# A decoder layer on one core: the input projection by seven half-size products, in a phase of its own

## The chip, the core and the metric

The kernel runs on one core of a Trainium2 chip. A core has five engines, each with its own instruction queue: TensorE (PE) for matmuls, with its weight loads as PEld; VectorE (DVE), ScalarE (ACT) and GpSimd (POOL) for work on 128 partitions; SyncE (SP), which here issues nearly all transfers between DRAM and the on-chip memory (SBUF), in order. An instruction waits on semaphores at the head of its engine's queue, and all that is queued behind it on that engine waits too. Matmuls write into banks of PSUM. The metric is the time of one execution on the device, in microseconds; lower is better.

## The reference

One layer for 1024 tokens of width 1024, all in fp32. `c` gives shifts, scales and gates; the mixer's input projection makes 62 chunks of 128 columns; two kinds of attention follow, gated branches, an output projection, layer norm, and a feed-forward part.

```python
u = x * (1.0 + scale_m) + shift_m
proj = einsum('btd,de->bte', u, w_in)              # 1024 x 1024 by 1024 x 7936
qa, ka, va, qb, kb, vb, ga, gb = split(proj)       # A: 16 query, 2 key/value heads; B: 3 groups of 8 heads
qa, ka, qb, kb = rope(...)                         # rotary embedding
oa = banded_window_attention(qa, ka, va, 127, sinks)
for g, (window, dil) in enumerate(((128, 1), (512, 4), (2048, 16))):
    o_g, lse_g = dilated_attention(q_g, k_g, v_g, window, dil)
ob = sum over g of softmax(lse)[g] * o_g
y  = (sigmoid(ga) * (oa @ w_branch_a) + sigmoid(gb) * (ob @ w_branch_b)) @ w_o
x  = layer_norm(alpha * x + (1 + gate_m) * y)
h  = (x * (1 + scale_f) + shift_f) @ w_gate_up     # then silu(hg) * hu, @ w_down
x  = layer_norm(alpha * x + (1 + gate_f) * ...)
```

## The kernel before

**Products.** TensorE takes fp32 numbers as a rounded part and a remainder ("hi" and "lo"). A product of two such numbers is three matmuls, hi·hi, hi·lo and lo·hi (`mac`, L136 to L139). A weight piece of 128x512 is loaded (`w_raw`, L55), copied to `w_hi` by ACT (L78) and its remainder `w_lo` made by DVE (L79). A chunk of the input projection is 8 slices of the inner dimension by two halves of the tokens by three: 48 matmuls with 512 columns.

**Prologue** (to about 72 us). It makes `u` from x as eight pairs of tiles, and the first three chunks (`EARLY`) beside it.

**Phase 1** (72 to about 834 us). Twenty units of attention, 12 of kind B (pair of heads p, group g with strides 1, 4, 16) and 8 of kind A, each in four sub-steps. `stream` yields the projection of the keys, values and queries of each unit in small pieces, and `pump` and `at` place these between the attention's instructions on PE so that a unit's projection runs while the unit before it attends. Rope is in `rotary`: a product with the cosines (DVE, L422), a shuffle (DVE, L423), a product with the sines and an addition that also reorders the columns by residue (POOL, L425, L426). `q_stacks` and `k_stacks` then write the hi and lo parts to partitions 0 to 63 and 64 to 127. Scores are L501 and L507, exponentials L528, transposes of the probabilities L550 with their copies L552, weighing of values L573. Results go to DRAM; group weights and row sums come back as broadcasts into `wb` by loads over 64 partitions each (`fetch_bcast`, L615).

**Phase 2** (to about 1117 us). Twenty-four branch steps (three blocks of eight columns chunks), between them 14 of 16 gates made by projection (`make_gate`, in a list `order`); two gates were made at the end of phase 1 and kept in DRAM (`ga_d`). One step of `ada` a branch step or gate forms later shifts and gates on DVE (`acc`, L826). Then the merged result `m` is split, in three blocks.

**The rest.** A pass over w_o, layer norm, and the feed-forward part. Its first projection already runs as seven products of half-size matrices per pair of chunks: `g_sums` forms sums of weight halves on POOL (L1080 to L1086), `g_split` makes their hi and lo parts, `product` (L1106) issues 12 matmuls, and the results are added.

The lines that the change rests on in PE's and SP's order:

```python
ends = np.cumsum(lengths)
at = lambda x: pump(min(int(start + (stop - start) * (i + x) / 4), total - 1))
scores(un, qr); at(0.4); turn_probs(*subs[s - 1]); exponentials(*subs[s]); at(0.8); weigh(...)
```

## Time and profile before

| what | value |
|---|---|
| times of two runs | 1898.89 and 1903.19 us, median 1901.04 |
| profiled execution: its own time | 1908.77 us |
| its span, first to last instruction | 1907.0 us |
| mean granted TensorE clock | 0.987 |
| PE busy | 1841.1 us (97%) |
| DVE busy | 1160.4 us (61%) |
| ACT busy | 782.0 us (41%) |
| POOL busy | 596.5 us (31%) |
| DMA | 170.83 MB, mean 90 GB/s |

"Busy" is the time in which an engine has an instruction of its own under way; what a busy PE does is not told by it. An idle stretch of PE is put down to what released the waiting instruction. A row of groups reads: line, engine, operation, tiles written <- read, shapes, count, then busy time in all, mean nanoseconds of one, idle time of the engine just before them with the releaser. In a table of windows each row gives start and end in microseconds, the length, each engine's busy time with its number of instructions, the granted clock (PEclk, 1.00 is full), the busy share of the 16 DMA engines and the rate. In a timeline the figures are start and duration, both in microseconds. Matmuls overlap, so their pitch is shorter than the duration of one.

### The profile page before, as it was taken

To read this page: it belongs to the slowest core of one execution; us is meant where nothing else is said; L and a number is where in the kernel's file an instruction comes from. 1 tells how busy PE (TensorE), PEld (TensorE's weight loads), DVE (VectorE), ACT (ScalarE), POOL (GpSimd) and SP (SyncE) were. 2 spreads that over 40 slices of the span, in tenths; PEclk is the share of its full clock that TensorE was granted. 3 is DMA by queue.
4 is the path that set the end of the run, shared out by engine and by line. 5 is a ranking of instruction groups with operands and counts; after the bars stand their busy time and mean duration, and the time that the engine had idled before them with its cause. 6 is when DMAs were issued, how large, how long until landed. Compare 5 with 4: busy or idle time off the path is not lost.

```text
span 1907.0 us, 24471 instructions
## 1 busy us (share of the span) xinstructions
PE 1841.1 (97%) x8988; PEld 1489.6 (78%) x8988; DVE 1160.4 (61%) x2161; ACT 782.0 (41%) x1661; POOL 596.5 (31%) x389
## 2 busy tenths in 40 slices
PE   6899999999999999989999999999999999899998
PEld 5688877878878777768888878778888888788886
DVE  7855667667677887534555364575565444565557
ACT  3455545445444767633122132653333333412122
POOL 2432223223323222100311142455664333431213
PEclk9899999999999999989999999999999999999999
DMA  8011112111121122254534123123222222432222
GB/s 316 28 34 34 40 41 74 45 57 56 41 63 50 53 89 68 79 178 164 175 118 161 56 75 124 56 89 100 89 78 89 78 89 95 135 125 90 93 71 89
DMA packets 72266, 170.83 MB, mean 90 GB/s; under 512 B 13073, under 2 KB 14161, under 8 KB 72146
## 3 DMA queue, kind: packets, MB, share of 16 engines
q1 hardware_dynamic: 71810, 168.21, 26.7%
q8 instruction: 71, 1.16, 0.3%
q0 software_dynamic: 336, 1.06, 0.2%
q14 instruction: 49, 0.40, 0.1%
HBM read 145.80 MB, written 23.43 MB: 89 GB/s over the span
## 4 chain that ended last, share of the span: by engine, by line
PE 51%; DVE 3%; ACT 1%; issue 1%; DMA 1%; SPq 0%; POOL 0%; DVEq 0%; ACTq 0%; POOLq 0%
PE pf L1106 21%; PE p L138 5%; PE p L139 5%; PE p L137 5%; PE pf L137 5%; PE pf L139 5%; PE pf L138 5%; DVE m L118 1%; DMA h_raw<-h_d 0%; DVE wd L79 0%; DVE h L118 0%; DMA oa_d<-o 0%; PE px L1034 0%; PE p L835 0%; PE p L842 0%
## 5 line engine op out<-in xcount | busy, mean ns | idle before, releaser
L137 PE MATMUL pj<-u,w_hi 128*128 128x512 f32 x720 | 301.5, 419 | 0.0
L139 PE MATMUL pj<-u,w_lo 128*128 128x512 f32 x720 | 283.9, 394 | 0.0
L138 PE MATMUL pj<-u,w_hi 128*128 128x512 f32 x720 | 282.6, 392 | 0.0
L425 POOL TENSOR_TENSOR rb<-rb,sin_t 128x512 f32<-128x512 f32 x64 | 86.8, 1356 | 502.0 <-DVE rb L423 431.5
L118 DVE TENSOR_TENSOR w_lo<-r,w_hi 128x512 fp32r<-128x512 f32 x110 | 117.7, 1072 | 138.7 <-ACT w_hi L117 137.9
L79 DVE TENSOR_TENSOR w_lo<-w_raw,w_hi 128x512 fp32r<-128x512 f32 x150 | 133.4, 893 | 85.3 <-ACT w_hi L78 83.0
L528 ACT ACTIVATE probs<-probs,st 128x128 f32<-128x128 f32 (+1 forms) x320 | 146.0, 461 | 60.5 <-DVE st L518 30.8
L137 PEld LDWEIGHTS pj<-u,w_hi 128*128 128x128 f32 x720 | 136.4, 189 | 33.6 <-issue 4.7
L139 PEld LDWEIGHTS pj<-u,w_lo 128*128 128x128 f32 x720 | 135.8, 189 | 30.7
L138 PEld LDWEIGHTS pj<-u,w_hi 128*128 128x128 f32 x720 | 136.7, 190 | 22.6
L137 PE MATMUL pf<-wd,h 128*128 128x512 f32 x352 | 139.2, 395 | 3.4 <-DVE zt L1326 2.9
L138 PE MATMUL pf<-wd,h 128*128 128x512 f32 x352 | 138.7, 394 | 1.9 <-DVE wd L79 1.9
L139 PE MATMUL pf<-wd,h 128*128 128x512 f32 x352 | 138.6, 394 | 0.0
L62 POOL TENSOR_TENSOR w_raw<-w_raw,gate 128x512 f32<-128x512 f32 x60 | 83.1, 1404 | 157.0 <-DMA w_raw<-in_w_down 134.4
L1326 DVE SCALAR_TENSOR_TENSOR zt<-zt,pf 128x512 f32<-128x512 f32 x112 | 76.2, 685 | 85.1 <-PE pf L139 85.0
L426 POOL TENSOR_TENSOR r<-ra,rb 128x512 f32<-128x512 f32 x63 | 114.5, 1817 | 6.1 <-DVE kl L460 1.3
L78 ACT ACTIVATE w_hi<-w_raw 128x512 fp32r<-128x512 f32 x150 | 92.0, 624 | 29.0 <-PE p L138 12.0
L552 ACT ACTIVATE ptsb<-pt 128x512 f32<-128x512 f32 (+1 forms) x128 | 63.6, 548 | 93.6 <-PE pt L550 93.2
L137 PE MATMUL p<-u,w_hi 128*128 128x512 f32 x224 | 88.3, 394 | 0.0
L139 PE MATMUL p<-u,w_lo 128*128 128x512 f32 x224 | 87.2, 389 | 0.0
L138 PE MATMUL p<-u,w_hi 128*128 128x512 f32 x224 | 87.2, 389 | 0.0
L137 PE MATMUL p<-o_hl,w_hi 128*128 128x512 f32 x192 | 75.9, 395 | 8.0 <-ACT o_hl L117 8.0
(297 smaller groups left out, 4267.2 us busy)
## 6 DMA issues: line engine op xcount, KB each, us to landing
w_raw<-in_w_in SPq DMA_DIRECT2D x118, 256.0 KB
r<-in_w_gate_up SPq DMA_DIRECT2D x47, 512.0 KB
a_raw<-in_w_ada SPq DMA_DIRECT2D x32, 512.0 KB
w_raw<-in_w_down SPq DMA_DIRECT2D x44, 256.0 KB
h_raw<-h_d SPq DMA_DIRECT2D x22, 512.0 KB
h_d<-g SPq DMA_DIRECT2D x40, 256.0 KB
wa<-in_w_ada_m SPq DMA_DIRECT2D x16, 512.0 KB
wb<-wt_d SPq DMA_DIRECT2D x24, 256.0 KB
```

Source lines behind the costliest of these rows:

```text
L62: self.nc.gpsimd.tensor_tensor(self.raws[i], self.raws[i], scale(), op=OP.mult)
L78: self.nc.scalar.activation(hi, raw, AF.Copy)
L79: self.nc.vector.tensor_tensor(lo, raw, hi, op=OP.subtract)
L118: nc.vector.tensor_tensor(lo, src, hi, op=OP.subtract)
L137: nc.tensor.matmul(ps, w[0], m[0], start=first, stop=False)
L138: nc.tensor.matmul(ps, w[0], m[1], start=False, stop=False)
L139: nc.tensor.matmul(ps, w[1], m[0], start=False, stop=last)
L425: eng.tensor_tensor(b, b, sin_t[:, s], op=OP.mult)
L426: eng.tensor_tensor(residue_half(res, r, t), by_residue(a, r), by_residue(b, r), op=OP.add)
L528: nc.scalar.activation(pr, pr, AF.Exp, bias=st[:, 0, h, b:b + 1], accum_out=st[:, 1, h, b:b + 1])
L1106: nc.tensor.matmul(ps, w[:, c], m[:, k], start=first and k == 0 and n == 0, stop=k == 3 and n == 2, skip_group_check=True)
L1326: nc.vector.scalar_tensor_tensor(z, z, ALPHA if gi == 0 else 1.0, pd, op0=OP.mult, op1=OP.add)
```

## The change

The 59 chunks of the input projection that follow the three early ones are taken apart from attention. Of them 52 are made in pairs by the seven products (a class `SevenProducts`, which the feed-forward part now shares): with the inner dimension and the tokens halved, seven products of 12 matmuls replace 96 matmuls by 84 for each pair of chunks. The operands made from `u` (sums and differences of its quarters: t1 to t4) are formed from x, which is loaded once more after the prologue, and split into hi and lo (`split_to`). One chunk of a pair (`ea`) is always a query or key chunk; the other a value or a gate chunk, or in five pairs another query or key chunk. Hi and lo parts of queries and keys (`hl_d`), the values (`v_d`) and nine gates (`ga_d`) are written to DRAM.

Then the attention phase begins. For each unit the query stacks (four loads of 64x1024), key stacks (four of 64x1024), the keys' remainders and the values are loaded, one unit ahead. Six gates are still made in full, woven between its sub-steps (48 pieces over 80 sub-steps), for which a quarter of `u` is formed once more. Probabilities are turned two sub-steps later instead of one, values weighed three later instead of two, and the PSUM banks are shared out anew. The last gate is made at the start of the branch phase, which otherwise has only the 24 branch steps, each with two steps of `ada`; gates are loaded, and `m` is split column chunk by column chunk in the last steps.

What moves in POOL's queue, in the kernel before, in the middle of phase 1 (`rb` and `ra` are the parts of rope, `r` its result):

```order
L426 TENSOR_TENSOR r<-ra,rb 128x16x32
L425 TENSOR_TENSOR rb<-rb,sin_t 128x512
L426 TENSOR_TENSOR r<-ra,rb 128x512
L425 TENSOR_TENSOR rb<-rb,sin_t 128x512
L426 TENSOR_TENSOR r<-ra,rb 128x512
```

And in the changed kernel, in one pair of the input phase; `half` and `row` are parts and results of rope, the tiles named r_ are raw weights and s_ their sums (957 and 959 of one pair, 1128 and 1130 of the next):

```order
L125 TENSOR_TENSOR s_1089<-s_1088,r_957 128x512
L591 TENSOR_TENSOR row<-half 128x512
L127 TENSOR_TENSOR r_959<-r_957,r_959 128x512
L531 TENSOR_TENSOR half<-half,sin_t 128x512
L534 TENSOR_TENSOR row<-half 128x16x32
L531 TENSOR_TENSOR half<-half,sin_t 128x512
L534 TENSOR_TENSOR row<-half 128x16x32
L123 TENSOR_TENSOR s_1259<-r_1130 128x512
L129 TENSOR_TENSOR r_957<-r_957,s_1089 128x512
L125 TENSOR_TENSOR s_1260<-s_1259,r_1128 128x512
```

POOL had only rope there; now the weight sums of the next pair and the fourth sum of the present one (L129) stand behind two halves of rope.

SP's queue in phase 1 of the kernel before, between two units (`st_d`, `cst` and `wb` carry group weights):

```order
L615 DMA wb<-wt_d 64x1024 x2
L55 DMA w_raw<-in_w_in 128x512
L664 DMA ob_d<-o 128x1024
L55 DMA w_raw<-in_w_in 128x512 x3
L590 DMA st_d<-sr 32x128
L55 DMA w_raw<-in_w_in 128x512 x6
```

And in the changed kernel where the input phase ends and attention begins (`qs`, `kh`, `kl`, `v` are the loads of the first unit, `ut` the quarter of x, `w_raw` the weights of the first woven gate):

```order
L503 DMA hl_d<-row 128x1024
L504 DMA hl_d<-row 128x1024
L627 DMA qs<-hl_d 64x1024
L628 DMA qs<-hl_d 64x1024
L627 DMA qs<-hl_d 64x1024
L628 DMA qs<-hl_d 64x1024
L615 DMA kh<-hl_d 64x1024 x4
L620 DMA kl<-hl_d 128x1024
L632 DMA v<-v_d 128x1024
L915 DMA ut<-in_xT 128x512 x4
L55 DMA w_raw<-in_w_in 128x512 x6
```

SP carried only weights there; now the first unit's ten loads stand behind the last stores, and the weights of the gate, with which PE's instructions of the new phase begin, behind those.

The diff, cut to its core:

```diff
+PRODUCTS = ("b11", "b21", "t2", "t1", "t3", "b22", "t4")
...
+class SevenProducts:
...
+    def load(self, p, both=True):
+        got = []
+        for i, src in enumerate(self.sources[p][:1 + both]):
+            got.append(self.pool.tile([P, T], F32, name=f"r{i + 1}", bufs=2))
+            self.nc.sync.dma_start(got[i], src)
+        self.raws[p] = got
+    def sums(self, p, step):
+        r1, r2 = self.raws[p]
+        tt = self.nc.gpsimd.tensor_tensor
+        if step == 0:
+            self.s[p] = [self.pool.tile([P, 512], F32, name=n, bufs=1) for n in ("s1", "s2")]
+            tt(self.s[p][0], r2[:, H0], r2[:, H1], op=OP.add)
+        elif step == 1:
+            tt(self.s[p][1], self.s[p][0], r1[:, H0], op=OP.subtract)
+        elif step == 2:
+            tt(r2[:, H0], r1[:, H0], r2[:, H0], op=OP.subtract)
+        else:
+            tt(r1[:, H1], r1[:, H1], self.s[p][1], op=OP.subtract)
+    def split(self, p, i):
+        raw = self.raws[p]
+        src = (raw[0][:, H1] if i in (1, 5) else raw[0][:, H0] if i == 0 else self.s[p][3 - i] if i in (2, 3) else
+               raw[1][:, H0 if i == 4 else H1])
+        hi, lo = [self.wpool.tile([P, 512], F32R, name=n, tag=n, bufs=4) for n in ("w_hi", "w_lo")]
+        self.split_(hi, lo, src)
+        self.ready.append((hi, lo))
+    def prepare(self, upto):
+        while self.prepared < min(upto, len(self.jobs)):
+            p, i = self.jobs[self.prepared]
+            if i == 5:
+                self.sums(p, 3)
+            self.split(p, i)
+            self.prepared += 1
+    def product(self, ps, i, first):
+        hi, lo = self.ready.pop(0)
+        b = self.B[PRODUCTS[i]]
+        for k in range(4):
+            c = slice(k * P, (k + 1) * P)
+            for n, (w, m) in enumerate(((hi, b[0]), (hi, b[1]), (lo, b[0]))):
+                self.nc.tensor.matmul(ps, w[:, c], m[:, k], start=first and k == 0 and n == 0,
+                                      stop=k == 3 and n == 2, skip_group_check=True)
...
-    tail_gates = (4, 5)
-    for e in range(EARLY, 46):
+    rope_chunks = [e for e in range(EARLY, 36) if e % 3 != 1] + [36] + list(range(38, 46))
+    other_chunks = [e for e in range(EARLY, 36) if e % 3 == 1] + [37] + list(range(46, 55))
+    pairs = []
+    while rope_chunks:
+        pairs.append((rope_chunks.pop(0), other_chunks.pop(0) if other_chunks and len(pairs) % 5 != 4
+                      else rope_chunks.pop(0)))
+    assert not other_chunks
+    woven_gates, last_gate = list(range(55, 61)), 61
+    for e in woven_gates + [last_gate]:
...
+    hl_d = dram.tile([46, 2, P, T], F32, name="hl_d")
+    v_d = dram.tile([13, P, NB, P], F32, name="v_d")
...
+    t_half = slice(TH, T)
+    for name in ("t2", "t1", "t4"):
+        operand(name, low1)
+    raw_t3 = [row() for _ in range(2)]
+    for k in range(4):
+        uab = []
+        for j in (k, k + 4):
+            x_t = row()
+            nc.sync.dma_start(x_t, I["xT"][j])
+            u_again(x_t, x_t, j, 0)
+            uab.append(x_t)
+        if k == 1:
+            inp.load(0)
+        ua, ub = uab
+        t3 = raw_t3[k // 2][:, (k % 2) * TH:(k % 2 + 1) * TH]
+        nc.gpsimd.tensor_tensor(t3, ub[:, t_half], ua[:, t_half], op=OP.subtract)
+        nc.vector.tensor_tensor(ua[:, t_half], ua[:, t_half], ua[:, :TH], op=OP.subtract)
+        nc.vector.tensor_tensor(ua[:, :TH], ub[:, t_half], ua[:, t_half], op=OP.subtract)
+        nc.vector.tensor_tensor(ub[:, :TH], ub[:, :TH], ua[:, :TH], op=OP.subtract)
+        for name, src in (("t2", ua[:, :TH]), ("t1", ua[:, t_half]), ("t4", ub[:, :TH])):
+            split_to(name, k, src)
...
+    def store_rope(e):
+        res = outs_of.pop(e)
+        hi, lo = row(F32R), row(F32R)
+        def first():
+            nc.scalar.activation(hi, res, AF.Copy)
+        def second():
+            nc.vector.tensor_tensor(lo, res, hi, op=OP.subtract)
+            nc.sync.dma_start(hl_d[e, 0], hi.bitcast(F32))
+            nc.sync.dma_start(hl_d[e, 1], lo.bitcast(F32))
+        soon(2, first)
+        soon(3, second)
...
+        if kind == "rope":
+            b = half()
+            nc.vector.stream_shuffle(b, src, SWAP16)
+            a = half() if in_psum else src
+            nc.vector.tensor_tensor(a, src, cos_t[:, c], op=OP.mult)
+            nc.gpsimd.tensor_tensor(b, b, sin_t[:, c], op=OP.mult)
+            if e not in outs_of:
+                outs_of[e] = row()
+            nc.gpsimd.tensor_tensor(residue_half(outs_of[e], r_of(e), t), by_residue(a, r_of(e)),
+                                    by_residue(b, r_of(e)), op=OP.add)
...
+    inp.jobs = [(p, i) for p in range(len(pairs)) for i in range(7)]
+    for step in range(3):
+        inp.sums(0, step)
+    inp.load(1)
+    inp.prepare(3)
+    for e in range(EARLY):
+        for t, ps in enumerate(early.pop(e)):
+            from_psum(e, t, ps)
...
+    for p, (ea, eb) in enumerate(pairs):
+        ps, kept = {}, {}
+        for i in range(7):
+            inp.prepare(n + 3)
+            bank = "abacaca"[i]
+            if bank not in ps:
+                pool, name = banks_of[bank]
+                ps[bank] = pool.tile([P, TH], F32, name=name)
+            x = ps[bank]
+            inp.product(x, i, i in (0, 1, 3))
+            n += 1
+            if i == 4 and p + 2 < len(pairs):
+                inp.load(p + 2)
+            if i in (0, 2, 3, 4):
+                kept[i] = half()
+                nc.scalar.activation(kept[i], x, AF.Copy)
+            if i in (1, 5):
+                t = i // 5
+                dst, order_ = target(ea, t)
+                nc.vector.tensor_tensor(dst, order_(kept.pop(i // 5 * 2)), order_(x), op=OP.add)
+                after(ea, t, dst)
+            if i == 4:
+                dst, order_ = target(eb, 1)
+                nc.gpsimd.tensor_tensor(dst, order_(kept.pop(4)), order_(kept.pop(3)), op=OP.add)
+                soon(1, lambda eb=eb, dst=dst: after(eb, 1, dst))
+            if i == 6:
+                from_psum(eb, 0, x)
+            if i in (2, 3, 4) and p + 1 < len(pairs):
+                inp.sums(p + 1, i - 2)
             tick()
+    while later:
+        tick()
+    ph1a.close()
...
+    def load_keys(e, both, box):
+        box["kh"] = [att.tile([P, T], F32R, name="kh", bufs=4) for _ in range(2)]
+        box["kl"] = [att.tile([P, T], F32R, name="kl", bufs=3) for _ in range(1 + both)]
+        for h, own in enumerate((LO, HI)):
+            for to in (LO, HI):
+                nc.sync.dma_start(box["kh"][h][to].bitcast(F32), hl_d[e, 0, own])
+            if both:
+                for to in (LO, HI):
+                    nc.sync.dma_start(box["kl"][h][to].bitcast(F32), hl_d[e, 1, own])
+        if not both:
+            nc.sync.dma_start(box["kl"][0].bitcast(F32), hl_d[e, 1])
+            box["kl"] *= 2
+    def load_queries(e, box):
+        box["q"] = [att.tile([P, T], F32R, name="qs", bufs=4) for _ in range(2)]
+        for h, own in enumerate((LO, HI)):
+            nc.sync.dma_start(box["q"][h][own].bitcast(F32), hl_d[e, 0, own])
+            nc.sync.dma_start(box["q"][h][(HI, LO)[h]].bitcast(F32), hl_d[e, 1, own])
...
+    def load_unit(n, part):
+        if n >= len(units):
+            return
+        un = units[n]
+        if "b" in un:
+            p, g = un["b"]
+            base = (p * 3 + g) * 3
+            if part == 0:
+                load_queries(base + 2, un["box"])
+                load_keys(base, False, un["box"])
+            else:
+                load_values(base + 1, un["box"])
...
+        for e in woven_gates:
+            g = att.tile([P, T], F32, name="g", bufs=2)
+            yield from project(lambda t, ps: sigmoid_half(g[:, t * TH:(t + 1) * TH], ps))
+            nc.sync.dma_start(ga_d[e - 46], g)
...
+    load_unit(0, 0)
+    load_unit(0, 1)
+    for x in range(2):
+        u_tiles[x, 1, 0] = bigu.tile([P, 4, TH], F32R, name=f"u{x}10", tag="big")
+    for k in range(4):
+        ut = att.tile([P, TH], F32, name="ut", bufs=2)
+        nc.sync.dma_start(ut, I["xT"][k][:, TH:])
+        u_again(ut, ut, k, 1)
+        split(u(0, 1, k), u(1, 1, k), ut)
+    pump(3)
+    for s in range(len(subs) + 3):
         n, i = divmod(s, 4)
-        start = ends[min(n, len(units) - 1)] + LEAD if n < len(units) else total
-        stop = ends[n + 1] + LEAD if n + 1 < len(units) else total
-        at = lambda x: pump(min(int(start + (stop - start) * (i + x) / 4), total - 1))
+        at = lambda x: pump(max(3, int(total * (s + x) / len(subs))))
+        if i in (0, 3):
+            load_unit(n + 1, i // 3)
...
+    for k in range(4):
+        o_part(0, k)
+    g_last = mix.tile([P, T], F32, name="gt", bufs=2)
+    ps = {t: ps_2.tile([P, TH], F32, name="p2") for t in range(2)}
+    for t in gemm_u(ps, ws.take(2), (1, 5)):
+        if t is not None:
+            sigmoid_half(g_last[:, t * TH:(t + 1) * TH], ps[t])
+    nc.sync.dma_start(ga_d[last_gate - 46], g_last)
...
+        if b < 2 and dc >= 3 and dc < 7:
+            o_part(b + 1, dc - 3)
+        if i + 1 >= 8 and i + 1 < len(steps):
+            make_gate(i + 1)
+        if i == 16:
+            mg, _ = wide("m", bigu)
         for t in range(2):
             merge(b, dc, t, ps[t], gts.get(i))
+        if i > 16:
+            split_merged(dc - 1)
         next(ada, None)
-        if i == 22:
-            split_merged(range(3, 6))
-    split_merged(range(6, 8))
+        next(ada, None)
+    split_merged(7)
```

389 lines of the change are left out of this document (148 added, 241 removed).

## Prediction

> **What bounds the kernel now.** I read the head of the page first, for the engine that is nearly never idle; then a table of windows, one per stage, for where TensorE (PE) does stand still; then the longest piece of the chain of waits, because the FFN already uses the seven products that the change brings to the input.
>
> ```profile
> span 1907.0 us, 24471 instructions
> PE 1841.1 (97%) x8988; PEld 1489.6 (78%) x8988; DVE 1160.4 (61%) x2161; ACT 782.0 (41%) x1661; POOL 596.5 (31%) x389
> core 0: us, PE busy (x) PEld busy (x) DVE busy (x) ACT busy (x) POOL busy (x), PEclk, DMA share, GB/s
> 72.00:100.00 28.00, 20.81 (x86) 16.51 (x85) 24.78 (x37) 13.85 (x22) 13.44 (x8) 0.82 0.06 20
> 100.00:820.00 720.00, 709.38 (x4050) 561.58 (x4049) 488.67 (x1258) 395.67 (x1036) 189.04 (x120) 1.00 0.18 56
> 820.00:845.00 25.00, 16.19 (x65) 12.34 (x64) 6.96 (x10) 7.00 (x10) 4.66 (x5) 0.86 0.68 226
> 845.00:1117.00 272.00, 272.00 (x1202) 224.18 (x1201) 128.57 (x161) 62.43 (x107) 47.04 (x29) 0.99 0.39 128
> 1248.90 388.72 PE pf L1106 x1702
> ```
>
> The windows run from the first projection matmul (72 us) to the pass over w_o (1117 us), which is the stretch that the change rewrites. PE is busy in all but 7.2 + 10.6 + 8.8 = 27 us of it, so a matmul less is time less, and any new wait of PE is time more. The chain's piece gives the price of a matmul of 128x512 in a dense run of seven products: 388.72/1702 = 0.228 us. PE's own timeline shows what a wait costs besides its length:
>
> ```profile
> 90.38 0.45 PE L501 MATMUL s<-kh,qs 128*128 128x128 f32 x1 [6.38 <-DVE qs L440]
> 94.28 0.63 PE L139 MATMUL pj<-u,w_lo 128*128 128x512 f32 x1
> 94.71 0.63 PE L137 MATMUL pj<-u,w_hi 128*128 128x512 f32 x1
> 95.13 0.63 PE L138 MATMUL pj<-u,w_hi 128*128 128x512 f32 x1
> 842.32 0.80 PE L137 MATMUL p<-o_hl,w_hi 128*128 128x512 f32 x1 [8.00 <-ACT o_hl L117]
> ```
>
> After 6.4 us without work the matmuls start 0.43 us apart, not 0.23, for some 9 matmuls, and for some 14 after the 8.0 us: 9 x 0.2 = 1.8 and 14 x 0.2 = 2.8 us. With these, the old stretch holds about 27 + 4.6 = 31 us that are not work at full clock, and the change does away with the places where they lie.
>
> **The change, part by part.**
>
> *Matmuls taken away.* From 72 us on, the kernel before makes 59 chunks of 48 matmuls, 2832. After it there are 26 pairs of 7 x 12 = 84, and 7 gates still made in full, 336: 2520. 312 fewer x 0.228 = **-71 us**. Everything else on PE (scores, transposes, weighing, branch products) stays in number. The 31 us of old waits go too: **-31**.
>
> *First gap: prologue to first product.* Before, the projection's first matmul follows the prologue's last directly. Now x is loaded again and four rounds make the operands t2, t1, t4.
>
> ```profile
> L265 ACT ACTIVATE ut<-xt,mod 128x1024 f32<-128x1024 f32 x4 | 4.9, 1236 | 10.0 <-issue 10.0
> L117 ACT ACTIVATE w_hi<-r 128x512 fp32r<-128x512 f32 x110 | 67.9, 620 | 1.9 <-PE pf L1106 1.3 <-POOL r L1086 0.5
> L79 DVE TENSOR_TENSOR w_lo<-w_raw,w_hi x150: 627/692/1936, 66.3 to 1146.5; 128x512 fp32r<-128x512 f32 x150
> ```
>
> A round on ACT is two full rows (2 x 1.24), then copies (0.62 each) that wait in turn for three dependent subtractions on VectorE (DVE), 0.69 each: 2.5 + 2.1 + 0.6 = 5.2 us, and the next round's rows stand behind the last copy in ACT's order. Four rounds from about 70 us end near 91; the first weight's split stands behind them all, so PE starts near 92: 20 us idle, 2.7 us at half clock. Then the first products wait some 5 us for sums which stand behind the three early chunks' rope on GpSimd (POOL): **+28** (between 22 and 35).
>
> *The 26 pairs.* A pair is 84 x 0.228 = 19.2 us of PE. POOL must do four weight sums in it, and rope for each q or k chunk.
>
> ```profile
> L1080 POOL TENSOR_TENSOR s<-r 128x512 f32<-128x512 f32 x22 | 28.4, 1291 | 86.6 <-DVE w_lo L118 81.1 <-issue 2.5 <-DMA r<-in_w_gate_up 2.3
> L1082 POOL TENSOR_TENSOR s<-s,r 128x512 f32<-128x512 f32 x22 | 31.6, 1438 | 1.7
> L1084 POOL TENSOR_TENSOR r<-r,r 128x512 f32<-128x512 f32 x22 | 37.5, 1706 | 0.0
> L1086 POOL TENSOR_TENSOR r<-r,s 128x512 f32<-128x512 f32 x22 | 30.3, 1378 | 0.0
> L425 POOL TENSOR_TENSOR rb<-rb,sin_t 128x512 f32<-128x512 f32 x64 | 86.8, 1356 | 502.0 <-DVE rb L423 431.5
> L426 POOL TENSOR_TENSOR r<-ra,rb 128x512 f32<-128x512 f32 x63 | 114.5, 1817 | 6.1 <-DVE kl L460 1.3
> L423 DVE STREAM_SHUFFLE rb<-pj 128x512 f32<-128x512 f32 x64 | 47.0, 735 | 0.0
> ```
>
> Sums 1.29 + 1.44 + 1.71 + 1.38 = 5.8 us; rope 2 x (1.36 + 1.82) = 6.3 us a chunk; one half-row addition about 1.3. A pair of a rope chunk with a value or gate chunk: 13.5 of 19.2 us. A pair of two rope chunks, of which there are 5: 19.8, over PE's time. Even a light pair meets POOL's order: the fourth sum, from which the sixth product's weight is split, stands behind a rope half. From the end of product 2: addition and shuffle on DVE 1.4, sine and addition 3.2, the fourth sum 1.4, split 1.2 to 2: 7.2 to 8.0 us, against 3 x 2.74 = 8.2 us until the sixth product. The rows for L426 mix a plain addition with strided ones, and where chunks are strided (14 pairs) about 0.4 us of wait follows. In a rope-rope pair POOL is 0.6 us over and the next pair's sums queue behind one more rope half; I take 1.7. So 14 x 0.4 + 5 x 1.7 = **+14**, between 0 (the FFN's pairs, with 193.83 us of POOL in the window of 388, run without a wait) and 26 x 1.3 = 34, every pair late by a w_lo at its longest (1.94 us for 0.63).
>
> *Second gap: last product to attention.* SP issues all of unit 0's loads behind the last store to DRAM, then four quarters of x, then the gate's weights, and PE's first instruction there is a gate matmul that needs those. Prices of transfers, first full-height ones in two stretches, then stretches in which the 64-partition loads of wb (L615) are in flight:
>
> ```profile
> 24.00:36.00 12.00, 11.06 (x38) 8.55 (x37) 11.68 (x18) 3.34 (x4) 3.76 (x3) 1.00 1.02 383
> 835.00:839.00 4.00, 0.00 (x0) 0.00 (x0) 0.00 (x0) 0.00 (x0) 1.81 (x2) 0.88 0.99 392
> 284.00:287.00 3.00, 2.12 (x19) 1.45 (x16) 2.92 (x13) 2.98 (x8) 0.00 (x0) 1.00 0.87 242
> 668.00:670.00 2.00, 2.00 (x18) 1.41 (x15) 2.00 (x4) 0.00 (x0) 0.00 (x0) 1.00 0.73 209
> ```
>
> The stores leave about 4.4 us after the last product (rope and its split). Then 2.1 MB in half-height pieces at 242 GB/s, 8.7 us, and 1.05 + 1.05 + 0.5 MB at 383, 6.8 us; with about 1.5 us for landing and split PE starts 21.5 us after its last product, and runs 2.5 us slow: **+24** (18 to 28).
>
> *Attention.* Its work on PE now: the first three windows hold 744 us up to 835 (I take 14 of the third window's as before it), less 2160 projection matmuls at 0.228 (492) and about 15 of value transposes and slow or first branch matmuls: 237 us for 20 units. With six gates woven in (288 x 0.228 = 66) it is 303. By share of their blocks a group of three B units needs about 42 us of PE, an A unit 16.8. Per group DMA brings 6.3 MB of half-height q and k, 1.6 MB of half-height wb, and about 4.2 MB full height: 7.9/0.242 + 4.2/0.383 = 43.6 us. So B is bound by transfers by a hair: 4 x 43.6 = 174 against 168. ACT is next:
>
> ```profile
> L528 ACT ACTIVATE probs<-probs,st 128x128 f32<-128x128 f32 (+1 forms) x320 | 146.0, 461 | 60.5 <-DVE st L518 30.8
> L528 ACT ACTIVATION_READ_ACCUMULATOR probs<-probs,st 128x1 f32 x320 | 60.9, 190 | 0.0
> L552 ACT ACTIVATE ptsb<-pt 128x512 f32<-128x512 f32 (+1 forms) x128 | 63.6, 548 | 93.6 <-PE pt L550 93.2
> ```
>
> 16 x (0.46 + 0.19) + about 3.7 = 14.1 us a unit: under 16.8, so A stays with PE. 6 us for B, 5 for the first unit whose chain has nothing in front of it, 4 for the drain at the end: **+15** (5 to 35).
>
> The Trainium skill ("SBUF — State Buffer", Door 1: The DMA port swizzle) says that a transfer over 64 partitions reaches 8 of 16 ports and measured 196 GB/s there. The rows' 209 to 249 lie above that, at a share under one; by the page's figure a group takes 7.9/0.196 + 11 = 51 us, the B part 205, and the sum below would be +18 instead of -13. This is weighed as rival C, at the rate that the rows show.
>
> *Branch phase.* The window 845 to 1117 moved 272 x 128 = 34.8 MB. The gates' weights (7.3 MB) leave it, the gates themselves (8.4 MB) come in from DRAM, and its PE time shrinks to some 145 us: 248 GB/s in the mean, where 383 to 392 is the most that a stretch showed. Two ada steps per branch step need 1 MB and 2.6 us of DVE:
>
> ```profile
> L826 DVE SCALAR_TENSOR_TENSOR acc<-a_raw,c_act,acc 128x1024 f32<-128x1024 f32 x28 | 37.0, 1323 | 8.0 <-DMA a_raw<-in_w_ada 8.0
> ```
>
> Already now 8 us of DVE's idle time wait for these loads. In the twelve steps where gates, ada and weights coincide I expect a little PE wait: **+8** (0 to 40).
>
> *At nothing:* the stores of q, k, v and gates, some 46 MB, with 27 MB of weights over 520 us 141 GB/s, under the 383 that a stretch showed; the negated maxima and sinks, merged into one DVE operation per step; and the split of m, now spread over the last eight branch steps, where DVE has room beside 5.5 us of PE a step. If that cover goes, DVE's 1.2 us per half of m is PE's wait, 10 us at most.
>
> *Sum:* -71 - 31 + 28 + 14 + 24 + 15 + 8 = **-13 us**. The profiled execution took 1908.77 us (its span of 1907.0 and 1.8 around it), 7.7 over the median of 1901.04; I apply the difference to the median: **1888**.
>
> **Rivals.** (The measurement tells 2%, 38 us, from no change: the bounds are 1863 and 1939.)
>
> A, *clean*: only the two gaps cost. POOL's and the branch phase's waits are covered by weights split two products ahead, as in the FFN where PE had 388.00 of 388 us busy in its dense window. Gaps 25 + 22, attention 5: -102 + 52 = -50, **1851**. For it: POOL's slack in 21 pairs. Against: the 7.2 to 8.0 us against 8.2 above.
>
> B, *pairs at POOL's pace*: DVE and POOL slow each other, and every pair is late by 1.3 us: 34 for 14, **1908**. The row of L79, from 0.63 to 1.94 us for one operation, is for it; that POOL has 5.7 us free in 21 of the pairs is against it. The Trainium skill ("SBUF — State Buffer", SBUF: two separate sides) has DVE and GpSimd share a port pair that one holds for a whole instruction while the other waits; the spread of the row agrees, and no row tells how often that would happen here.
>
> C, *half-height loads rule* (the other side): in the attention's B part every transfer, full or half, runs at the rate of the mixed stretch, 209 GB/s, since all share one queue and the halves alternate. 12.1 MB a group are then 58 us, 14.4 more than I took, 4 x 14.4 = 58: **1946**. It decides once the mean rate falls below 12.1 MB/42 us = 288 GB/s. For it: no stretch with such loads shows over 249. Against: in none of them did the queue have work all the time (share 0.73 to 0.87).
>
> The forecast is that the new gaps and waits eat some seven eighths of the 102 us.
>
> **How the numbers follow.** Chances: forecast 0.53, A 0.24, B 0.10, C 0.13. Faster than 1863 comes from nearly all of A and a little of the forecast: 0.25. Slower than 1939 from three quarters of C and a twentieth of the others: 0.14. The rest, 0.61, is within. The low end takes in A with a short gap more off, 1845; the high end B and the half of C, 1935.
>
> **What would show it.** In the profile after: PE idle of about 20 us ahead of the first L153 matmul and about 21 ahead of the first L196 of attention, each followed by spacing of 0.43; the pieces of L153 between them 500 to 530 us long; PE waiting for splits of the sixth product (its source a POOL sum, L129) about half a microsecond in strided pairs, up to 2 in rope-rope ones; in attention's B part a DMA share near one, groups of 43 to 45 us, and in its A part PE over 95%; in the branch phase waits that end with gt or a_raw. A DMA share near one with groups of 55 us or more means C; pairs of 21 us mean B; pairs of 19.3 and groups of 42 mean A. The forecast falls if either gap is half or twice as long, or if the branch phase waits over 30 us.

## The result and the profile after

The changed kernel takes 2149.88 us (2149.61 to 2150.14, two runs) against 1901.04 before: the ratio is 1.131, with a 95% interval of 1.125 to 1.136. Forecast were 1888 us and no measurable change. The head of the page and the table of windows by stage, of the changed kernel (windows: start and end, length, busy time of PE, PEld, DVE, ACT and POOL with instructions, granted clock, DMA share, GB/s):

```profile
span 2147.8 us, 24759 instructions
PE 1859.1 (87%) x8676; PEld 1483.7 (69%) x8676; DVE 1245.0 (58%) x2179; ACT 848.4 (40%) x1839; POOL 827.9 (39%) x527
```

```profile
72.00:101.00 29.00, 0.00 (x0) 0.00 (x0) 20.31 (x31) 17.73 (x27) 8.80 (x7) 0.52 0.32 122
101.00:727.00 626.00, 552.00 (x2286) 433.40 (x2287) 409.58 (x478) 220.44 (x380) 421.72 (x258) 0.95 0.29 112
727.00:758.00 31.00, 0.82 (x4) 0.38 (x3) 5.65 (x9) 8.71 (x13) 2.76 (x2) 0.58 0.72 212
758.00:1177.00 419.00, 329.97 (x2157) 252.09 (x2158) 190.78 (x856) 255.40 (x869) 0.00 (x0) 0.85 0.65 165
1177.00:1368.00 191.00, 163.58 (x664) 130.46 (x663) 115.81 (x123) 44.17 (x67) 54.07 (x37) 0.91 0.61 213
1368.00:2147.00 779.00, 760.37 (x3354) 625.69 (x3353) 452.28 (x597) 271.39 (x449) 318.30 (x206) 0.99 0.28 94
```

PE has 312 instructions fewer than before (8676 for 8988), as counted, and yet is busy 18 us longer: many matmuls run at half clock, and in the attention the granted clock is 0.85. And it stands still for about 290 us of the span, where it stood still for 66.

Set beside the forecast, each stage between its first matmul and the first of the next, from PE's timeline:

| stage | forecast | measured | miss |
|---|---|---|---|
| start of the first product | 92 | 101 | 9 |
| the 26 pairs, first to last product | 530 | 626.5 | 96 |
| gap to the attention phase | 21.5 | 30.2 | 9 |
| attention | 318 | 419.0 | 101 |
| branch phase | 153 | 191.5 | 38 |
| from w_o on | as before, 790 | 779.5 | -10 |

The forecast entries are those of the prediction's terms: 499 for the products with 14 of waits, 5 at the start, about 12 for value transposes and slow clock; 303 + 15; 145 + 8. The misses add to 243 us. The spans differ by 240.8 where -13 was forecast, which is 254; the other ten lie in the forecast itself, whose stages add up to 1904.5 us and whose sum gives 1894. Two terms, the pairs and the attention, hold four fifths of the error.

Who PE waited for, in the changed kernel (total in us, times, longest):

```profile
PE po L153 <- ACT half L583: 53.3, 25, 4.9
PE pt L771 <- DVE es L765: 32.2, 7, 9.5
PE pj L153 <- DVE half L530: 31.0, 1, 31.0
PE pj L196 <- ACT w_hi L78: 30.2, 1, 30.2
PE pt L751 <- ACT ptsb L716: 18.3, 7, 5.9
PE s L665 <- DVE mx L677: 15.8, 5, 5.7
PE pj L153 <- DVE w_lo L177: 15.4, 11, 2.9
PE p L1017 <- DVE acc L1001: 10.7, 2, 7.3
PE p L1010 <- DVE acc L1001: 8.0, 2, 6.3
```

The first row is a wait once a pair, at the sixth product (`po`). One pair's timeline shows where it comes from; its first row is the last matmul of the second product:

```profile
304.94 0.39 PE L153 MATMUL s<-u,w_lo 128*128 128x512 f32 x1
306.31 0.68 DVE L587 TENSOR_TENSOR half<-half,s 128x512 f32<-128x512 f32 x1
307.84 1.80 POOL L531 TENSOR_TENSOR half<-half,sin_t 128x512 f32<-128x512 f32 x1 [5.77 <-DVE half L528]
309.72 2.39 POOL L534 TENSOR_TENSOR row<-half 128x512 f32<-128x512 f32 x1
312.07 1.28 POOL L123 TENSOR_TENSOR s<-r 128x512 f32<-128x512 f32 x1
313.31 1.26 POOL L129 TENSOR_TENSOR r<-r,s 128x512 f32<-128x512 f32 x1
314.60 0.63 ACT L176 ACTIVATE w_hi<-r 128x512 fp32r<-128x512 f32 x1 [5.92 <-POOL r L129]
315.14 0.58 ACT L583 ACTIVATE half<-po 128x512 f32<-128x512 f32 x1
315.77 1.22 PE L153 MATMUL po<-u,w_hi 128*128 128x512 f32 x2 [2.28 <-ACT half L583]
```

It is a chain, of which the row of waits names only the last link: rope's product and addition, the next pair's first sum (L123), this pair's fourth sum (L129), its split on ACT, and behind that split, in ACT's order, the copy of product 4 out of the bank into which product 6 adds.

### The profile page after: what moved, and what is told of

It reads as the page before. It is cut to its first block, busy times and chain, and to the rows that moved or that the text cites. A ratio compares the mean times of both kernels' runs of the same rounds, so it can differ in the third digit from the quotient of the medians.

```text
span 2147.8 us, 24759 instructions
## 1 busy us (share of the span) xinstructions
PE 1859.1 (87%) x8676; PEld 1483.7 (69%) x8676; DVE 1245.0 (58%) x2179; ACT 848.4 (40%) x1839; POOL 827.9 (39%) x527
## 4 chain that ended last, share of the span: by engine, by line
PE 44%; DVE 16%; DMA 12%; POOL 10%; issue 9%; ACT 8%; SPq 2%; DVEq 0%; POOLq 0%; ACTq 0%
PE pf L153 19%; PE pf L196 4%; PE pf L197 4%; PE pf L198 4%; POOL half L531 3%; PE po L153 3%; DMA a_raw<-in_w_ada 3%; POOL row L534 3%; DVE w_lo L177 2%; DVE half L528 2%; DMA kl<-hl_d 2%; DMA wb<-wt_d 2%; PE pt L714 2%; ACT probs L692 2%; POOL s L123 2%
## 5 line engine op out<-in xcount | busy, mean ns | idle before, releaser
L177 DVE TENSOR_TENSOR w_lo<-r,w_hi 128x512 fp32r<-128x512 f32 x240 | 296.5, 1245 | 253.1 <-ACT w_hi L176 252.7
L176 ACT ACTIVATE w_hi<-r 128x512 fp32r<-128x512 f32 x240 | 146.6, 623 | 164.0 <-POOL r L129 163.6
L531 POOL TENSOR_TENSOR half<-half,sin_t 128x512 f32<-128x512 f32 x66 | 114.5, 1735 | 176.2 <-DVE half L528 176.2
L534 POOL TENSOR_TENSOR row<-half 128x512 f32<-128x512 f32 x66 | 132.5, 2008 | 5.2
L153 PE MATMUL po<-u,w_hi 128*128 128x512 f32 x208 | 83.2, 488 | 53.3 <-ACT half L583 53.3
L177 DVE TENSOR_TENSOR w_lo<-s,w_hi 128x512 fp32r<-128x512 f32 x96 | 73.4, 771 | 88.4 <-ACT w_hi L176 87.4
L123 POOL TENSOR_TENSOR s<-r 128x512 f32<-128x512 f32 x48 | 64.4, 1342 | 84.9 <-DVE w_lo L177 81.1
L714 PE MATMUL pt<-ident,probs 128*128 128x128 f32 x520 | 84.1, 306 | 9.4 <-ACT ptsb L716 9.2
L153 PE MATMUL pj<-u,w_hi 128*128 128x512 f32 x208 | 65.1, 395 | 31.0 <-DVE half L530 31.0
L198 PE MATMUL p<-o_hl,w_lo 128*128 128x512 f32 x192 | 78.6, 409 | 6.6 <-DVE w_lo L79 6.6
L714 PEld LDWEIGHTS pt<-ident,probs 128*128 128x128 f32 x520 | 64.8, 155 | 21.7 <-ACT ptsb L716 10.5
```

The source lines that it names most:

```text
L123: tt(self.s[p][0], r2[:, H0], r2[:, H1], op=OP.add)
L153: self.nc.tensor.matmul(ps, w[:, c], m[:, k], start=first and k == 0 and n == 0, stop=k == 3 and n == 2, skip_group_check=True)
L176: nc.scalar.activation(hi, src, AF.Copy)
L177: nc.vector.tensor_tensor(lo, src, hi, op=OP.subtract)
L198: nc.tensor.matmul(ps, w[1], m[0], start=False, stop=last)
L531: nc.gpsimd.tensor_tensor(b, b, sin_t[:, c], op=OP.mult)
```

## The experiments

All stage times below are read in the same way as in the table above, each from one execution. Where an edit does not touch them, the pairs took 625 to 631 us, the attention 415 to 419 and the branch phase 190 to 194 (196 to 198 in runs with full-height loads), so a few microseconds in one stage show no effect. Two theories for each stage were set against each other.

**The pairs: order or throughput?** First the fourth sum alone was issued earlier:

```diff
     def prepare(self, upto):
             p, i = self.jobs[self.prepared]
-            if i == 5:
+            if i == 3:
                 self.sums(p, 3)
```

> One thing moves: each pair's fourth weight sum (L129 of the changed kernel) is issued on GpSimd two products earlier, ahead of the rope operations of the first half instead of behind them. Theory ORDER: TensorE waits before the sixth product of each pair only because this sum stands behind rope and the next pair's first sum in GpSimd's queue; the stretch of 626 us from the first to the last product then shrinks to 520 to 550 us, waits of po for ACT half nearly vanish, and the whole goes from 2150 to 2045 to 2075 us. Theory THROUGHPUT (rival B): GpSimd's work, about 17 us a pair and slowed by VectorE, is simply too much, in whatever order; the stretch stays above 600 us and the whole above 2125 us.

Measured: 2107.0 us; pairs 589.4 for 626.5. The feed-forward part uses the same class, so its sums moved too, and its first pair's fourth sum was left out; from w_o on it took 779.7 us for 779.5, so this does not touch the comparison. The wait at `po` went from 53.3 to 3.9 us, so the order was a cause, worth 37 us; but the stretch, though under the rival's 600, stayed far from 520 to 550. What had been hidden behind it is seen in VectorE's weight remainders (128 of those read from raw weights), in the pairs' stretch of the changed kernel and of this run:

```profile
L177 DVE TENSOR_TENSOR w_lo<-r,w_hi 128x512 fp32r<-128x512 f32 x128 | 178.1, 1406 | 114.7 <-ACT w_hi L176 114.7
```

```profile
L177 DVE TENSOR_TENSOR w_lo<-r,w_hi 128x512 fp32r<-128x512 f32 x128 | 224.4, 1788 | 4.1 <-ACT w_hi L176 3.9
```

The same subtraction takes 1.406 us in the mean in the changed kernel and 1.788 in this run: with the order mended, GpSimd is busy in 75% of the stretch for 67%, and VectorE slows with it. In this run PE waits for these remainders, and for ACT's copies, while ACT itself stands 130 us for results of GpSimd's rope:

```profile
PE pj L153 <- DVE w_lo L177: 24.1, 19, 3.8
PE pj L153 <- ACT half L583: 16.9, 21, 1.5
```

In the next run, GpSimd has nothing to do in that stretch, and the fourth sum is early too:

```diff
-        tt = self.nc.gpsimd.tensor_tensor
+        tt = self.eng.tensor_tensor                 # VectorE in the input phase
...
-            nc.gpsimd.tensor_tensor(b, b, sin_t[:, c], op=OP.mult)
+            nc.vector.tensor_tensor(b, b, sin_t[:, c], op=OP.mult)
...
-            nc.gpsimd.tensor_tensor(residue_half(outs_of[e], r_of(e), t), ...)
+            nc.vector.tensor_tensor(residue_half(outs_of[e], r_of(e), t), ...)
...
-                nc.gpsimd.tensor_tensor(dst, order_(kept.pop(4)), ...)
+                nc.vector.tensor_tensor(dst, order_(kept.pop(4)), ...)
```

> In the input phase all of GpSimd's work (four weight sums a pair, rope's product and addition, the half-row addition of the second chunk) runs on VectorE, and the fourth sum is issued early as in the run before it (the feed-forward part is left as it was). Theory CONTENTION: with the sum early, the pairs still take 22.6 us because VectorE's subtractions take 1.7 us in place of 0.69 whenever GpSimd runs; alone, VectorE has about 7 x 0.69 for weight remainders, 4 x 0.69 for sums and some 9 us for the rest, 16 to 17.5 us a pair, under TensorE's 19.2; the stretch from first to last product falls to 510 to 545 us and the whole to 2030 to 2065. Rival LOAD: VectorE is 79% busy already, and seven to nine more operations a pair make it the bound: pairs of 23 us or more, the whole at or above 2107.

The pairs' stretch of this run, as a window and by its weight remainders:

```profile
100.00:632.00 532.00, 514.70 (x2288) 420.64 (x2288) 459.69 (x738) 223.21 (x380) 0.00 (x0) 1.00 0.36 132
```

```profile
L178 DVE TENSOR_TENSOR w_lo<-r,w_hi 128x512 fp32r<-128x512 f32 x128 | 87.8, 687 | 6.1 <-ACT w_hi L177 5.3
```

Measured: 2051.9 us; pairs 531.8. VectorE does all of GpSimd's work besides its own (738 instructions for 478) and is busy 459.7 us, only 50 more than the 409.6 of the changed kernel, because its own operations are shorter: a weight remainder takes 0.69 us again. PE is busy 514.7 of 532 us at full clock. So 37 us of the excess went with GpSimd's order and a further 58 us when its work moved to VectorE; what is left is the forecast's own length. The run takes away two things at once, the slowing of the two engines by each other and the waits of ACT and VectorE for results from GpSimd; their shares of the 58 are not separated.

**The attention: half-height loads or the order of waits?** The loads were made full-height by storing queries and keys in the stacked form:

```diff
-            nc.sync.dma_start(hl_d[e, 0], hi.bitcast(F32))
-            nc.sync.dma_start(hl_d[e, 1], lo.bitcast(F32))
+            # keys: each half of hi twice, in stacks of 128 rows, and lo; queries: hi to rows 0:64 and 192:256, lo to 64:192
...
-            for to in (LO, HI):
-                nc.sync.dma_start(box["kh"][h][to].bitcast(F32), hl_d[e, 0, own])
+            nc.sync.dma_start(box["kh"][h].bitcast(F32), kh_d[e, h])
...
-            nc.sync.dma_start(box["q"][h][own].bitcast(F32), hl_d[e, 0, own])
-            nc.sync.dma_start(box["q"][h][(HI, LO)[h]].bitcast(F32), hl_d[e, 1, own])
+            nc.sync.dma_start(box["q"][h].bitcast(F32), kh_d[e, h])
```

> Queries and keys are stored to DRAM in the stacked form in which attention needs them, so that each of its loads fills 128 partitions (two loads of 512 KB in place of four of 256 KB); the bytes loaded stay the same, stores are 4 and 5 a chunk in place of 2 where they were half-height before, in the input phase. Theory HALF-HEIGHT (rival C): B's units, 20.2 us apart now, are set by loads that reach 215 GB/s with a full queue; full-height loads bring them to 13 to 15.5 us, the attention phase from 419 to 335 to 365 us, the whole to 2065 to 2100 us. Rival WAITING ORDER: the units are late because broadcast loads stand behind the unit's loads on SP and because of the longer lags on ACT; then units stay above 18.5 us and the whole above 2125 us.

Measured: 2115.3 us; attention 382.8 for 419.0. The price of half-height loads stands in one window of the changed kernel, in which only such loads (of the first unit's queries and keys) run and the queue is full; then two windows of this run with the same unit's full-height loads, and the first three sends of statistics in SP's queue, of the changed kernel and of this run:

```profile
736.00:744.00 8.00, 0.00 (x0) 0.00 (x0) 0.00 (x0) 0.00 (x0) 0.00 (x0) 0.50 1.03 216
```

```profile
734.00:738.00 4.00, 0.00 (x0) 0.00 (x0) 0.00 (x0) 0.00 (x0) 0.00 (x0) 0.50 1.00 313
738.00:742.00 4.00, 0.00 (x0) 0.00 (x0) 0.00 (x0) 0.00 (x0) 0.00 (x0) 0.50 1.02 409
```

```profile
783.42 0.32 SPq L754 DMA_DIRECT2D st_d<-sr  x1
797.05 0.32 SPq L754 DMA_DIRECT2D st_d<-sr  x1
810.33 0.32 SPq L754 DMA_DIRECT2D st_d<-sr  x1
```

```profile
776.59 0.32 SPq L761 DMA_DIRECT2D st_d<-sr  x1
790.23 0.32 SPq L761 DMA_DIRECT2D st_d<-sr  x1
803.50 0.32 SPq L761 DMA_DIRECT2D st_d<-sr  x1
```

Each B unit sends its statistics (`st_d`) once. The first sends, before anything is combined, follow each other at 13.6 and 13.3 us here, but they do so in the changed kernel too: there half-height loads alone did not hold the units back. Over all twelve the pitch is 17.7 us (20.2 in the changed kernel), so the gain comes where weights are broadcast as well. There VectorE stands in its queue for the broadcasts, in the changed kernel and in this run:

```profile
DVE o L824 <- DMA wb<-wt_d: 47.5, 6, 13.7
```

```profile
DVE o L831 <- DMA wb<-wt_d: 35.7, 7, 10.8
```

So both theories hold a part.

The A units by themselves: sums transposed one sub-step later, so that making and transposing them no longer share a sub-step.

```diff
-        if "a" in last and i == 2:
+        if "a" in last and i == 3:
             send_sums(last["a"])
-        if "a" in last and i == 3:
-            fetch_bcast(last["a"], wa_d[last["a"]])
...
-        if "a" in last and i == 0:
-            scale_a(last["a"])
+        if "a" in last and i == 0:                  # of the unit before it
+            fetch_bcast(last["a"], wa_d[last["a"]])
+        if "a" in last and i == 1:
+            scale_a(last["a"])
```

> In the eight A units the transposes of the row sums (L771) are issued one sub-step later than the operations that make them, with the broadcast and the scaling moved behind in the same way. Theory SAME SUB-STEP: TensorE waits 3 to 10 us a unit there because the change's longer lag put the making and the transposing of the sums into one sub-step; A units, 19.7 us apart, go to 16 to 17.5, the whole falls by 18 to 32 us to 2118 to 2132. Rival: ACT sets A's pace anyway (14 us of exponentials and copies and 2 of weight splits a unit), the wait only moves to the next instruction, and the whole falls by less than 8 us.

Measured: 2151.6 us; attention 413.3 (the pairs, which the edit does not touch, took 631.0 here, 4.5 more). The rival's outcome came: the wait of PE for `es` fell only from 32.2 to 24.0 us, and VectorE now waits 22.9 us for the broadcast sums (`wb`). Its reason, ACT's pace, is not shown by this.

Then both together, with the applications two sub-steps behind their loads and the small transposes in a bank of the scores:

```diff
+ full-height loads
-            if i:
-                combine_apply(p, i - 1)
+            if i > 1:
+                combine_apply(p, i - 2)             # the third in the next unit
...
-        pt = ps_t.tile([P, 4, P], F32, name="pt")   # send_stats, send_sums
+        pt = ps_s.tile([P, 4, P], F32, name="s")
```

> Full-height loads of queries and keys as before, and three moves in the attention phase alone: the broadcast group weights and row sums are applied two sub-steps behind their loads in place of one, the A units' sums are transposed one sub-step later, and the small transposes use a bank of the scores. Theory WAITING ORDER beside HALF-HEIGHT: what is left after full-height loads is VectorE standing in its queue for a broadcast load (30 us in B) and TensorE for a PSUM bank (17 us); B units go from 17.7 to 13 to 14.5 us, A units from 20 to 16 to 17.5, attention from 383 to 310 to 335 us, the whole to 2040 to 2070. Rival: the waits only move to the next instruction in the chain of maxima, exponentials and copies; attention stays above 365 us, the whole above 2095.

Measured: 2088.5 us; attention 353.1, between the two expectations. Then the loads of all units but the first two were left out:

```diff
+        if "b" in un and n >= 2:
+            un["box"] = units[n - 2]["box"]         # no loads
...
-                load_queries(36 + un["a"] + 2 * (un["a"] > 0), un["box"])
+                un["box"]["q"] = units[n - 2]["box"]["q"]
```

> The attention phase of the earlier combined run (full-height loads, later applications), but only the first two units load their queries, keys and values; the others use these tiles again, so 32 MB of loads are left out and the outputs are not those of the reference; every operation on the engines stays. Theory TRANSFERS: what is left over TensorE's own work in that run (353 us of attention for about 300 of work) is still the loads; attention falls to 300 to 320 us. Rival CHAIN: it is the chain from scores over maxima, exponentials, transposes and copies to the weighing, with SP's small transfers in it; attention stays above 340 us.

Measured: 2070.6 us; attention 332.6, again between the two expectations. So from 419 us: 36 went with the half-height loads, 30 with the places of waits, 20 with the loads at full height, and 332.6 are left without the units' loads. In these PE is busy 298 us, at a granted clock of 0.95, near the 303 of the forecast, and stands still for some 34; that these are a chain going round over all engines is not shown.

**The gaps.** The first gate's weights were fetched during the last pair and that gate made ahead of the scores:

```diff
+    ws.send()
+    ws.prepare(2)
     while later:
         tick()
...
+    # three of the four quarters of x are loaded ahead of load_unit(0, ...)
-    pump(3)
+    pump(8)
```

> The weights of the first woven gate are loaded and split during the last pair, x's quarter is loaded ahead of the first unit, and one whole gate (8 of 48 pieces) is made before the first scores; nothing else differs. Theory: the gap of 30 us after the last product is SP's order alone; the gate (11 us) runs in it, and what is left of it is 14 to 20 us ahead of the first scores, as unit 0's 3 MB take 14 us behind the last store; the whole falls by 10 to 16 us, to 2134 to 2140. Rival: the early gate only takes away work that filled TensorE's waits later in the attention phase, which transfers set; the whole falls by less than 5 us.

Measured: 2149.1 us; the gap fell from 30.2 to 7.5, the attention, which is counted from its first matmul, rose from 419.0 to 439.6. The rival's outcome came, a fall of less than 5 us, but not for its reason. The rise is one wait in the middle of the early gate:

```profile
PE pj L196 <- ACT g L475: 21.1, 1, 21.1
```

Three quarters of x are loaded ahead of the first unit, but the fourth, for which no buffer is free, stands behind that unit's loads; ACT waits for it, and the gate's second half for ACT. The gap was cut in two. The first scores came 44.8 us after the last product for 36.7, and from them to the end the attention took 402.3 us for 412.5, with 7 us less of the gate's work in them.

**The branch phase.** First more room between the last addition of an ada sum and its matmuls:

```diff
+                yield                               # two empty steps more
+                yield
             if m in (2, 5):
```

> Each of the four ada sums gets two empty steps between its last addition on VectorE and the matmuls that read it; nothing else differs. Theory: the branch phase (191 us for 149 us of work) is late because TensorE stands behind additions that wait for their loads (19 us in four places, with slow clock behind them); it shrinks by 12 to 25 us and the whole falls to 2125 to 2138. Rival TRANSFERS: the loads of gates, ada and weights set the pace of the whole phase; the waits turn up at the branch weights in place of the sums and the whole falls by less than 6 us.

Measured: 2144.5 us; branch phase 188.5 for 191.5. The wait only moved: at the sums it fell from 18.7 to 9.6 us, and for the branch weights' remainders it rose from 6.6 to 17.9. Then, without three quarters of the ada loads (the sums are not the reference's):

```diff
-                    raws[k] = mix.tile(...); nc.sync.dma_start(raws[k], ...)
+                    # loaded for k < 2, then raws[k] = raws[k - 2]
```

> The changed kernel, but of each ada sum's eight loads of 512 KB only two are made and their tiles used four times, so that 12 MB are left out and the sums are not those of the reference; all of VectorE's additions stay. Theory TRANSFERS (the branch phase waits for its loads, which stand in SP's queue behind ada loads that wait for one of two buffers): the branch phase falls from 191 to 150 to 165 us, the whole to 2105 to 2125. Rival VECTOR (VectorE's two additions a step, 2.6 of 5.5 us, and what stands behind them set the pace): it stays above 180 us.

Measured: 2119.6 us; branch phase 165.0, with 120.2 us of VectorE's work in it, more than the 115.8 before. It is the loads, be it by their bytes or by their place in SP's queue.

**All cures at once**, and two variants. The first holds the sums early and on VectorE, the attention's edits, the early gate and the ada steps apart:

> All four together, with the first gate made in the second gap. If the causes are separate and add up: -100 (pairs), -85 to -105 (attention), -12 to -25 (branch phase), -10 (gap): 1910 to 1945 us, still not under the kernel before. If one of them only hid another, it stays above 1965 us.

Measured: 1974.4 us; pairs 533.5, gap 6.4, attention 366.6, branch phase 188.1. That is above both 1945 and the 1965 that was to mean that one cause hid another. But the four runs by themselves saved 98, 61, 5 and 1 us, 165 together, and this one 176: the causes add up, and what was expected too large was the share of the attention and of the branch phase. The attention is 13.5 us longer than with the gap left alone, because the wait in the middle of the early gate (13.8 us here) counts in it.

With two gates made in the first gap (their matmuls between the four rounds, in PSUM banks of the transposes):

> All the earlier cures together, and two of the six woven gates made in the first gap, while the operands of the seven products are formed: theory: TensorE's work of 22 us moves from the attention phase into a gap of 28 us in which it stood still; the gap may grow by 2 to 4 us (their weight splits stand on ACT and VectorE ahead of the rounds), attention falls by 12 to 22; the whole goes from 1974 to 1952 to 1965 us. Rival: in attention TensorE waits for others, the gates there filled holes, and the whole stays above 1968.

Measured: 1972.4 us; the first product moved from 99.8 to 112.0, the attention from 366.6 to 359.2. So 22 us of PE's work taken out of the attention shortened it by 7 and cost 12 in the first gap; the other stages gave 7, and the whole fell by 2.

Last, the same with the ada loads on GpSimd's queue (`nc.gpsimd.dma_start`), timed in three rounds:

> The run with all cures and two gates in the first gap, and the ada loads issued on GpSimd's queue in place of SP's. Theory SP'S ORDER: the branch phase is late because weights, gates and attention's results stand in SP's queue behind ada loads that wait for one of two buffers; on another queue the same bytes cost little: the branch phase goes from 187 to 160 to 172 us and the whole from 1972 to 1945 to 1960 us. Rival BYTES: the transfers themselves, 1 MB of ada a step beside gates and weights, set the pace; the phase stays above 180 us and the whole above 1964. Under either the whole stays slower than the kernel before, 1901, by 2 to 4%.

Measured: 1994.7 us, ratio to the kernel before 1.051 (1.048 to 1.053); branch phase 202.5 for 186.7. Another queue did not help, but this does not clear SP's order: in the trace GpSimd's issues wait 49 us for VectorE to give a buffer back, with its own additions behind them, so the hold only moved to another queue. No version made here is faster than the kernel before.

## Why the prediction was wrong

**The saving was right.** 312 matmuls fewer are 71 us at the forecast's price, and that price holds: with GpSimd idle the stretch of pairs holds 514.7 us of PE for 26 x 19.2 and the values' transposes. It was spent in other places, and every term for these was too small: the measured stage less the forecast's work is about 110 us for the +14 of the pairs, 116 for the +15 of the attention and 46 for the +8 of the branch phase.

**"From the end of product 2 ... 7.2 to 8.0 us, against 8.2."** This step failed, and with it +14 and its upper end 34. The timeline of the pair above shows 10.6 us (product 2 gave way to the third at 305.2, the sixth started at 315.77). Three things were missing: the next pair's first sum, 1.28 us, stands ahead of the fourth in the very queue that was quoted; the shared durations (sine 1.80 for 1.36, addition 2.39 for 1.82) were taken from a phase in which GpSimd was busy a quarter of the time (189 of 720 us); and VectorE started 1.1 us late behind a w_lo. The upper end took one slow w_lo a pair; in the run with the sum early 128 of them, five a pair, took 1.79 us in the mean.

Rival B named that mechanism and priced it at 34 where order and contention together cost about 95. The Trainium skill ("SBUF — State Buffer", SBUF: two separate sides) has these two engines exclude each other for whole instructions, where VectorE's operation has two inputs in SBUF and GpSimd's reads from it; the runs agree: a remainder took 0.687 us in the mean with GpSimd idle, 1.41 and 1.79 with it busy 67% and 75% of the time. The 128 remainders so took 178.1 us in the changed kernel for 87.8, and the trace of before had the spread of 0.63 to 1.94 us to say so.

**Attention, +15.** The price of a half-height load was taken from windows in which such loads shared the queue with others: 242 GB/s. Alone with a full queue they make 216. Rival C had this mechanism, at 209 GB/s and 58 us a group; the measured groups are 3 x 20.2 = 61. It was given 0.13. The Trainium skill ("SBUF — State Buffer", Door 1: The DMA port swizzle) gives about 218 GB/s as the limit for 64 partitions; in the section "Can I just issue two DMAs to hit both halves?" the same page of the Trainium skill says that transfers to the two halves do not add up. The window of 216, in which the halves alternate, agrees with both; two windows of the full-height run show 313 and 409.

But the full-height run also shows that C was only 36 of the 101 us. The step that failed here is that the forecast took the attention as bound by the larger of two totals, transfers or PE's work, and had no term for what stands behind a late transfer: VectorE's maxima behind an application of weights that have not come, and ACT's exponentials behind those. VectorE's waits for broadcasts were 12.0 us in the trace of before:

```profile
DVE o L624 <- DMA wb<-wa_d: 6.0, 2, 5.4
DVE o L660 <- DMA wb<-wt_d: 6.0, 4, 1.7
```

They are 54.3 in the changed kernel (47.5 and 6.8 for the row sums), 22.7 with full height and later applications, and 3.6 without the units' loads:

```profile
DVE o L831 <- DMA wb<-wt_d: 3.6, 2, 2.0
```

ACT's waits for the maxima go along, from 60 to 89 and back to 59 us. So it is the units' loads, new in this phase, that make the broadcasts late. That the 2160 projection matmuls between the pieces of the chain, for which the change left 288, were cover as well is argued: the nearest run is the one in which 22 us of gates taken out of the attention shortened it by only 7. How much of the 101 us is lost cover no run shows.

**Branch phase, +8.** The miss is 38 us, so that the term came out at 46, beyond its range of 0 to 40. The mean rate of 248 GB/s was worked out, set against the 383 of a short stretch and so taken for covered. It is the ada loads: without three quarters of them the phase takes 165.

**Gaps, 28 and 24.** Each was 9 us short. In the first, a round took 6.82 us, not 5.2: the subtraction for t3 on GpSimd (1.26 us) heads each round and was not in the sum, though the diff has it:

```profile
76.10 1.26 POOL L447 TENSOR_TENSOR row<-row 128x512 f32<-128x512 f32 x1 [5.57 <-ACT row L430]
82.92 1.26 POOL L447 TENSOR_TENSOR row<-row 128x512 f32<-128x512 f32 x1 [5.56 <-ACT row L430]
```

And the first product did not wait for its weight but for its PSUM bank, which an early chunk's rope still held (`half` L530 in the list of waits). In the second, SP was held for 13 us by the third quarter of x, for which there are only two buffers:

```profile
739.93 13.16 SPq L915 DMA_DIRECT2D ut<-in_xT  x4
753.14 1.37 SPq L55 DMA_DIRECT2D w_raw<-in_w_in  x3
```

**The range.** 1845 to 1935 took every term as if the others stayed at their values. They fail together: each new wait lengthens the time in which PE runs at half clock, and only the terms of the two gaps had that in them. In the pairs alone PE is busy 552 us in the changed kernel and 515 with GpSimd idle, for the same matmuls: 37 us, which go with a granted clock of 0.95 for 1.00.

What stays open is the last 34 us of the attention without loads, and why the branch phase, with DMA busy 61% of the time, is slowed by bytes: that only two ada loads have a buffer is one possible reason, and no run has more.

## What to carry to other kernels

Work that is taken off the bound engine can also have been the cover of what was woven with it: before counting the saving, list each chain that it hid and price it without that cover. Count every instruction in an in-order queue between a producer and its reader, also those of the next iteration, and take durations from a stretch in which the neighbours are as busy as they will be. Price a transfer from a window in which that shape alone fills the queue.

## What the runs showed of the hardware

A wait of 2.3 us can be enough for the slow clock. After the wait in the pair shown above, matmuls that are 0.23 us apart start 0.43 us apart for 3 us:

```profile
316.79 0.63 PE L153 MATMUL po<-u,w_lo 128*128 128x512 f32 x1
317.22 1.05 PE L153 MATMUL po<-u,w_hi 128*128 128x512 f32 x2
318.07 0.63 PE L153 MATMUL po<-u,w_lo 128*128 128x512 f32 x1
319.18 0.39 PE L153 MATMUL po<-u,w_lo 128*128 128x512 f32 x1
```

It is not so after each: behind a longer wait, two pairs earlier, the spacing is 0.23 us from the fourth matmul on:

```profile
268.78 0.73 PE L153 MATMUL po<-u,w_hi 128*128 128x512 f32 x2 [2.87 <-ACT half L583]
269.52 0.50 PE L153 MATMUL po<-u,w_lo 128*128 128x512 f32 x1
269.86 0.62 PE L153 MATMUL po<-u,w_hi 128*128 128x512 f32 x2
270.32 0.39 PE L153 MATMUL po<-u,w_lo 128*128 128x512 f32 x1
```

Short waits that come back with every pair so cost more than their length: in the pairs' stretch the granted clock was 0.95, and 1.00 with GpSimd idle; PE stood still 74 us (626 - 552) against 17 (532 - 515), and on top of these 57 us came the 37 us by which it was busy longer.

GpSimd's help can be negative. With 422 us of its work in the pairs' stretch VectorE was busy 410 us; with all of that work on VectorE itself, and the fourth sum early, it was busy 460, and the stretch was 95 us shorter.
